# Rotary halves swapped by copies out of PSUM, the compression's sums moved forward, and the first head tile in the filling bank, in a two-layer hybrid attention kernel

## The chip, the cores and the metric

One core of one Trainium2 chip runs the whole program. The metric is the device time of one launch in microseconds (us): 1656.5 us is the median of 3 runs of the kernel before (1655.12 to 1657.21). Engines are named as the profile names them: PE (TensorE, matmul; PEld its weight loads), DVE (VectorE), ACT (ScalarE), POOL (GpSimd) and SP (SyncE, which here only issues DMAs).

## The reference, cut to what matters

Two layers of a hybrid block on 512 tokens of 1024 channels, all in float32. Only the part around the change is shown; the second attention (stick breaking), the merge and the convolutional feed-forward stay as they are.

```python
def rope(x, positions):                       # halves of 32 channels of each 64-channel head
    x1, x2 = xf[..., :half], xf[..., half:]
    return concatenate([x1 * cos - x2 * sin, x2 * cos + x1 * sin])

def compress_blocks(k, pe, w1, b1, w2):       # blocks of 32 tokens, stride 16
    blocks = k[:, idx] + pe
    return gelu(flat @ w1 + b1) @ w2

def hybrid_mixer(h, ...):
    q_nsa, kv_nsa, g_nsa, qkv_sb, g_merge = split(h @ w_in)
    q_nsa, k_cmp, k_slc, k_win = (rope(...) for the 8 query heads and 3 x 2 key heads)
    o_nsa = nsa_attention(...)                # compressed + selected + window branches, gated
    o_sb = stick_breaking_attention(...)
    return (sigmoid(g_a) * (o_nsa @ w_proj_nsa) + sigmoid(g_b) * (o_sb @ w_proj_sb)) @ w_out

for l in range(2):
    x = x + rms_norm(hybrid_mixer(rms_norm(x)))
    x = x + rms_norm(conv_ffn(rms_norm(x)))
```

## The kernel before, in words

Activations lie with channels on the 128 partitions and the 512 tokens along the free axis. Every large matmul is done as three (high times high, low times high, high times low), after a split of each 128x1024 block of weights into whi (ACT, L105) and wlo (DVE or POOL, L106). All matmuls are recorded at L382, in the helper `mm`; a projection of one 128x512 output tile is a "gemm" of 24 matmuls. So the trace is best read by tile names.

A layer starts with six **head tiles**, whose matmuls go in two halves of the tokens: two key tiles k1 and k2 (L644 and after, `k_tile`), two query tiles (`q_tile`), the compression's key tile (`kc_done`) and its value tile (written to `kd` at L677). They take the six PSUM banks of the pool `pg` (tag "bk"). Ahead of the loop the list of banks is turned by one (L565): the first head tile gets the second bank, and the last one gets the first.

Then come, in PE's order: `acc4`, four banks of 24 matmuls of 280 columns each (values and gate logits, 96 matmuls); two more query tiles (two gemms); and `cps`, two banks with 32 small matmuls each 132 columns wide, which sum the compression's windows from `cst`, the split copy of `cstk` (L712 ACT, L713 DVE). `cstk` is filled from `kd` by DMAs that SP issues (L660).

**rope** (L610) is run for seven tiles per layer, 14 in all. ACT copies the 128x512 bank to `rf` in SBUF (L616), which frees the bank once the copy is read out; SP issues four DMAs that write the four 32-partition blocks to `rs` in swapped order (L619); DVE multiplies `rf` by the cosines (L620) and, later, `rs` by the sines (L623); then sums and splits for k or q follow.

From the compression on, the attention is interleaved with **filling gemms**: projections for the second attention (`sb_pair`, read out by DVE at L781 as sbz) and for the merge's gates (`gate`, read out by DVE at L802). They all use one PSUM bank with the tag "f", the filling bank, so that a filling gemm can only start when the last one's bank has been read. The norm's sums in front of a layer use that tag, too, and in the second layer the last down-projection tiles of layer 0 (read by ACT at L1260) use the bank tags that the head tiles take over.

`cps` is read by ACT (`cpart`, L738), then by DVE (L739 and L740, `csum`), for two values of v in turn; `cpart` has one buffer.

The order of instructions on each engine isn't the order of the code: a scheduler sorts the recorded instructions by due times and costs, and `tc.high_priority()` pulls what is recorded in it forward. Each engine then runs its own list in order. When the bank a tile uses, or a priority, is changed, rows move on all engines, in the attention behind the change as well.

Lines that the steps below speak of: L561 `bank`, L564 and L565 the list of banks, L610 to L630 `rope`, L704 to L708 the reads of acc4 (vN, gates), L712 and L713 cst, L735 to L740 cpart and csum, L781 and L802 the reads of the filling bank, L859 to L870 the softmax of the compressed branch (cp, cm).

Of the kernel before, what the change touches and what calls it, by code (L numbers as in the profile page):

```python
# [9 lines left out]
F = mybir.dt.float32  # L10
# [20 lines left out]
HEAD = 6  # L31
# [127 lines left out]
def run_kernel(ctx, tc, xT, pos, inv, vec, pew, cw1, w_m, w_vn, w_pr, w_o, w_u, w_d, xmid, rot, out):  # L159
    nc = tc.nc  # L160
    uid = [0]

    def nm(s):
        uid[0] += 1
        return f"{s}_{uid[0]}"
# [56 lines left out]
    def act(out_, in_, fn, **kw):  # L222


        load_table(fn)
        op = nc.scalar.activation(out_, in_, fn, **kw)  # L226
        after(op, table["load"])
        table["users"].append(op)
# [134 lines left out]
    @contextmanager  # L363
    def temps(n):

        nonlocal tp_, n_tmp
        with pool("tp") as p:
            tp_, n_tmp = p, n
            yield p

    def wk(name, dt=F):
        return tp_.tile([128, T], dt, name=name, tag="tmp", bufs=n_tmp)
# [11 lines left out]
    def fbank(name):  # L384
        return ps1.tile([128, T], F, name=nm(name), tag="f" if name == "f" else "g", bufs=1)
# [138 lines left out]
    for l in range(DEPTH):  # L524
# [35 lines left out]
        def bank():  # L560
            return pg.tile([128, T], F, name=nm("bk"), tag="bk", bufs=6)  # L561


        banks = [bank() for _ in range(HEAD)]  # L564
        banks = banks[1:] + banks[:1]  # L565
        with temps(0) as hp:
            if l == 0:
                W.ensure(1)
# [12 lines left out]
        with temps(6) as ip:  # L581
# [6 lines left out]
            cosT, sinT = cs_t[:, 0], cs_t[:, 1]  # L588
# [21 lines left out]
            def rope(b, done):  # L610


                f = wk(nm("rf"))
                s_ = wk(nm("rs"))
                t = wk(nm("rt"))
                nc.scalar.copy(f, b)  # L616
                for p in range(4):
                    q = p ^ 1
                    nc.sync.dma_start(s_[p * 32:p * 32 + 32], f[q * 32:q * 32 + 32])  # L619
                nc.vector.tensor_mul(t, f, cosT)  # L620

                def rest():
                    nc.vector.tensor_mul(s_, s_, sinT)  # L623
                    done(t, s_)

                later.append(rest)

            def q_tile(p, b):
                def done(o, s_):
                    nc.vector.tensor_add(o, o, s_)  # L630
                    for e in range(2):
                        r = slice(e * 64, e * 64 + 64)
                        ro = slice(64 - e * 64, 128 - e * 64)
                        d = qs(2 * p + e)
                        nc.scalar.activation(d[r], o[r], AF.Copy, scale=0.125)
                        nc.vector.scalar_tensor_tensor(d[ro], o[r], 0.125, d.bitcast(F)[r], op0=OP.mult,
                                                       op1=OP.subtract)

                rope(b, done)

            def k_tile(br, b):
                def done(o, s_):
                    nc.vector.tensor_add(o, o, s_)
                    o = o.rearrange("p (j k) -> p j k", j=4)  # L644
                    for g in range(2):
                        r = slice(g * 64, g * 64 + 64)
                        ro = slice(64 - g * 64, 128 - g * 64)
                        hi, lo = (kdup(g, part).rearrange("p (j b k) -> p j b k", j=4, b=2)[:, :, br]
                                  for part in range(2))
                        nc.scalar.copy(hi[r], o[r])  # L650
                        nc.vector.tensor_sub(lo[r], o[r], hi.bitcast(F)[r])
                        both = kst[g].bitcast(F).rearrange("p (a b k) -> p a b k", a=8, b=2)[:, :, br]
                        nc.sync.dma_start(both[ro], both[r])

                rope(b, done)
# [11 lines left out]
            for i in head_second(banks, kept, n_pre=HEAD):  # L667
                b = banks[i]
                if i < 2:
                    k_tile(i, b)  # L670
                elif i < 4:
                    q_tile(i - 2, b)
                elif i == 4:
                    rope(b, kc_done)
                else:
                    mr = lambda a: a.rearrange("p (m r) -> p m r", r=2)
                    nc.vector.tensor_mul(kd[:, 1].rearrange("p r m -> p m r"), mr(b), mr(r2))  # L677
                    spread(1)
                flush_later(1)
# [5 lines left out]
            for n_kt in (3, 3, 2):  # L685
                hi, lo = W.get()
                for j in range(4):
                    tk = slice(j * 128, j * 128 + 128)
                    for q in range(n_kt):
                        a, b = hi[:, q * 280:q * 280 + 280], lo[:, q * 280:q * 280 + 280]  # L690
# [25 lines left out]
            for p in (2, 3):  # L716
                b = bank()
# [4 lines left out]
            cps = [bank(), bank()]  # L722
# [10 lines left out]
            hrep = aux[:, 320:576].rearrange("p (g a n) -> p g a n", g=2, a=4)  # L733
            nc.gpsimd.tensor_copy(aux[:, :192], PW[:64, 32:])
            for v in range(2):  # L735
                part = ip.tile([64, 132], F, name=nm("cpart"), tag="cpart")
                sums = ip.tile([64, 66], F, name=nm("csum"), tag="csum")
                nc.scalar.copy(part, cps[v][64:128, :132])  # L738
                nc.vector.tensor_add(part, cps[v][:64, :132], part)  # L739
                nc.vector.tensor_add(sums, part[:, :66], part[:, 66:])  # L740
                hb = ip.tile([64, 1], F, name=nm("hb"))
                nc.vector.tensor_add(hb, sums[:, 64:65], b1(v))
                act(hid[:, v], sums[:, 0:64], AF.Gelu_apprx_tanh, bias=hb)
# [384 lines left out]
        with temps(5) as yt:  # L1128
# [7 lines left out]
            with pool("py", space=PSUM) as py:  # L1136
# [18 lines left out]
                for m in projection(gb, s_hi, s_lo):  # L1155
                    t = wk(nm("yb"))
# [7 lines left out]
                def out_tile(m, tr, wt, side=None):  # L1164
                    b = bank()
                    w_ = tr.stop - tr.start
                    drain(gemm(b[:, :w_], wt, *y_of(tr), range(KD)), side)
                    return b[:, :w_]
# [10 lines left out]
                for m in range(n0):  # L1179
                    b = out_tile(m, ALL, W.get())  # L1180
# [3 lines left out]
                for m in range(n0, 8):  # L1184
                    kept[m] = W.get()
                    b = out_tile(m, HALVES[0], kept[m])
# [7 lines left out]
                for i, m in enumerate([6, 7, 2, 3, 4, 5]):  # L1194
                    b = out_tile(m, HALVES[1], kept[m], side)
# [11 lines left out]
            banks = [bank() for _ in range(HEAD)]  # L1207
# [9 lines left out]
        with temps(5) as ft_:  # L1217
# [24 lines left out]
            for i in range(HEAD, 2 * NF):  # L1242
                b = bank()
# [114 lines left out]
```

## Time and profile before

| what | value |
|---|---|
| median of 3 runs | 1656.5 us (1655.12 to 1657.21) |
| the profiled execution | 1653.88 us, of which the span on the engines is 1652.2 us; mean granted TensorE clock 0.989 |
| PE busy | 1609.0 us (97% of the span), 8970 matmuls |
| DVE, ACT, POOL busy | 1118.2 us (68%), 825.3 us (50%), 211.1 us (13%) |
| chain that ended last | PE 82%, DVE 8%, ACT 5%, DMA 2% |
| granted TensorE clock in 40 slices | 9 or more everywhere, but a little lower in the third slice (82 to 124 us) |
| DMA | 159.42 MB, mean 96 GB/s; 56 rotary swaps of 64 KB among them |

How to read it: PE is the bound. Since its instructions are in a fixed list, time is only lost where PE waits (an idle time in its timeline, with what released it) or where it runs at a lower granted clock (the clock column of a window: 1.00 is 2.4 GHz, 0.50 is 1.2 GHz). The busy time of another engine matters only where PE waits for it. Stretches named below: layer 0's head, acc4 and query tiles 28 to 80 us, its compression and attention 80 to 280 us; layer 1's the same from about 828, 895 us on.

### The profile page before, as it was taken

The numbers are of one execution on the slowest core, as the hardware profiler recorded it, in microseconds if no ns is written. First come the engines' busy times: TensorE is split into PE (matmuls) and PEld (weight loads), VectorE is DVE, ScalarE is ACT, GpSimd is POOL, SyncE is SP. The second block draws the span as 40 slices with busy tenths as digits, with TensorE's granted clock in tenths as the row PEclk, the third lists the DMA queues.
The fourth block names the chain that finished last, engine by engine and source line by source line (L and its number), as shares of the span: only waits on it lengthen the run. The fifth ranks groups of instructions, "written<-read, shape, count | busy, mean of one in ns | idle before, by whom it ended". The sixth has DMA issues, their size and how long they took to land.

```text
span 1652.2 us, 23212 instructions
## 1 busy us (share of the span) xinstructions
PE 1609.0 (97%) x8970; PEld 1393.2 (84%) x8970; DVE 1118.2 (68%) x1659; ACT 825.3 (50%) x1338; POOL 211.1 (13%) x252
## 2 busy tenths in 40 slices
PE   9899999999999999999999999999999999999997
PEld 9878887888998888888998788878889988888896
DVE  8775676767578777733677666677676687776235
ACT  6555565654555444423555455575536454444233
POOL 0034442120000000000000453322200000000000
PEclk9989999999999999999999999999999999999999
DMA  6521112114412233333664211112153132322344
GB/s 228 152 77 52 39 39 64 52 64 141 132 61 88 91 102 91 97 93 107 195 204 129 71 44 47 39 64 64 52 180 114 39 99 93 102 91 95 98 128 141
DMA packets 53501, 159.42 MB, mean 96 GB/s; under 512 B 6544, under 2 KB 12176, under 8 KB 53392
## 3 DMA queue, kind: packets, MB, share of 16 engines
q1 hardware_dynamic: 51088, 152.00, 29.0%
q0 software_dynamic: 1296, 4.72, 0.8%
q8 instruction: 70, 1.15, 0.3%
q10 hardware_dynamic: 1008, 1.23, 0.3%
q14 instruction: 39, 0.32, 0.1%
HBM read 144.30 MB, written 4.72 MB: 90 GB/s over the span
## 4 chain that ended last, share of the span: by engine, by line
PE 82%; DVE 8%; ACT 5%; issue 2%; DMA 2%; POOL 1%; SPq 1%; ACTq 0%; DVEq 0%; POOLq 0%
PE bk L382 56%; PE f L382 15%; PE pv L382 3%; PE Z L382 3%; PE S L382 2%; PE tp L935 2%; POOL sbt L1034 1%; DVE wlo L106 1%; DVE st L906 1%; DMA rs<-rf 1%; DMA x<-in_xT 1%; ACT whi L105 0%; ACT sbt L226 0%; ACT sbt L1058 0%; ACT sbw L226 0%
## 5 line engine op out<-in xcount | busy, mean ns | idle before, releaser
L105 ACT CAST whi<-wraw 128x1024 fp32r<-128x1024 f32 (+2 forms) x235 | 241.2, 1027 | 342.7 <-PE bk L382 254.3
L106 DVE TENSOR_TENSOR wlo<-wraw,whi 128x1024 fp32r<-128x1024 f32 (+2 forms) x209 | 248.8, 1191 | 184.1 <-ACT whi L105 181.4
L382 PE MATMUL bk<-h_hi,whi 128*128 128x512 f32 (+1 forms) x768 | 286.5, 374 | 2.1 <-ACT f_t L1260 1.7
L382 PE MATMUL bk<-h_hi,wlo 128*128 128x512 f32 (+1 forms) x768 | 286.4, 374 | 0.0
L382 PE MATMUL bk<-h_lo,whi 128*128 128x512 f32 (+1 forms) x768 | 286.2, 373 | 0.0
L382 PE MATMUL f<-h_hi,whi 128*128 128x512 f32 x448 | 184.4, 412 | 11.7 <-DVE gate L802 9.2
L382 PE MATMUL f<-h_lo,whi 128*128 128x512 f32 x448 | 179.1, 400 | 0.0
L382 PE MATMUL f<-h_hi,wlo 128*128 128x512 f32 x448 | 178.6, 399 | 0.0
L382 PEld LDWEIGHTS bk<-h_hi,whi 128*128 128x128 f32 x768 | 145.6, 190 | 27.7 <-ACT f_t L1260 1.9
L382 PEld LDWEIGHTS bk<-h_hi,wlo 128*128 128x128 f32 x768 | 145.5, 190 | 25.4 <-DVE wlo L106 0.4
L382 PEld LDWEIGHTS bk<-h_lo,whi 128*128 128x128 f32 x768 | 145.6, 190 | 24.8
L382 PE MATMUL bk<-ah,wlo 128*128 128x256 f32 (+1 forms) x484 | 161.7, 334 | 2.4 <-DVE wlo L106 2.4
L382 PE MATMUL bk<-ah,whi 128*128 128x256 f32 (+1 forms) x484 | 160.4, 331 | 0.0
L382 PE MATMUL bk<-al,whi 128*128 128x256 f32 (+1 forms) x484 | 160.2, 331 | 0.0
L382 PEld LDWEIGHTS f<-h_hi,whi 128*128 128x128 f32 x448 | 86.4, 193 | 30.6 <-DVE gate L802 10.0
L382 PEld LDWEIGHTS bk<-ah,wlo 128*128 128x128 f32 x484 | 91.8, 190 | 12.5 <-DVE wlo L106 3.4
L1228 DVE TENSOR_TENSOR cu<-bk,r 128x512 f32<-128x512 f32 x88 | 60.2, 687 | 61.2 <-PE bk L382 60.9
L382 PEld LDWEIGHTS f<-h_hi,wlo 128*128 128x128 f32 x448 | 85.9, 192 | 18.5
L382 PEld LDWEIGHTS f<-h_lo,whi 128*128 128x128 f32 x448 | 86.5, 193 | 15.5
L382 PEld LDWEIGHTS bk<-ah,whi 128*128 128x128 f32 x484 | 91.9, 190 | 8.7
L382 PEld LDWEIGHTS bk<-al,whi 128*128 128x128 f32 x484 | 91.9, 190 | 8.7
L382 PE MATMUL bk<-h_hi,wh 128*128 128x256 f32 x512 | 96.0, 285 | 0.0
(241 smaller groups left out, 3174.3 us busy)
## 6 DMA issues: line engine op xcount, KB each, us to landing
wraw<-in_w_u SPq DMA_DIRECT2D x88, 512.0 KB, 3.5
wraw<-in_w_m SPq DMA_DIRECT2D x72, 512.0 KB, 3.3
wraw<-in_w_d SPq DMA_DIRECT2D x44, 512.0 KB, 3.5
wraw<-in_w_d SPq DMA_DIRECT2D x22, 384.0 KB, 3.1
wraw<-in_w_pr SPq DMA_DIRECT2D x16, 512.0 KB, 3.6
wraw<-in_w_o SPq DMA_DIRECT2D x16, 512.0 KB, 3.5
rs<-rf SPq DMA_DIRECT2D x56, 64.0 KB, 2.8
wraw<-in_cw SPq DMA_DIRECT2D x4, 512.0 KB, 4.6
```

Source lines behind the costliest of these rows:

```text
L105: self.nc.scalar.copy(hi[:, c], raw[:, c])
L106: eng.tensor_sub(lo[:, c], raw[:, c], hi.bitcast(F)[:, c])
L382: last_mm[0] = nc.tensor.matmul(o, a, b, start=first, stop=last, skip_group_check=True)
L906: nc.vector.tensor_reduce(self.st[:, 0:2], self.S[:, :self.n].rearrange("p (j b k) -> p b j k", j=self.i + 1, b=2), axis=AX.XY, op=OP.max, ...
L935: nc.tensor.transpose(tp[:, b * 128:(b + 1) * 128], self.P[:, (c + b) * 128:(c + b + 1) * 128], ident)
L1034: nc.gpsimd.affine_select(out=d, in_=d, compare_op=OP.is_gt, fill=0.0, base=0, pattern=[[1, 128]], channel_multiplier=-1)
L1228: nc.vector.tensor_mul(u, b, r2)
```

## The change

Three edits. (1) rope drops `rf` and the DMAs: four ACT copies of 32 partitions each read the bank in swapped order and write `rs`, and DVE's multiplication by the cosines reads the bank itself. The bank is free when the copies and the multiplication have read it. (2) The first head tile goes into the filling bank, so that only five of the six banks are taken, and the list isn't turned. (3) `cpart` gets two buffers, and its copy and sum are recorded with high priority. Lines below the first edit move up by 1 to 3 (L619 and L620 become L616 and L617, L704 is L701, L712 is L709, L738 is L736, L781 is L779, L802 is L800, L863 is L861, L906 is L904).

```diff
--- before.py
+++ after.py
@@ -561,8 +561,7 @@
             return pg.tile([128, T], F, name=nm("bk"), tag="bk", bufs=6)
 
 
-        banks = [bank() for _ in range(HEAD)]
-        banks = banks[1:] + banks[:1]
+        banks = [fbank("f")] + [bank() for _ in range(HEAD - 1)]
         with temps(0) as hp:
             if l == 0:
                 W.ensure(1)
@@ -610,14 +609,12 @@
             def rope(b, done):
 
 
-                f = wk(nm("rf"))
                 s_ = wk(nm("rs"))
                 t = wk(nm("rt"))
-                nc.scalar.copy(f, b)
                 for p in range(4):
                     q = p ^ 1
-                    nc.sync.dma_start(s_[p * 32:p * 32 + 32], f[q * 32:q * 32 + 32])
-                nc.vector.tensor_mul(t, f, cosT)
+                    nc.scalar.copy(s_[p * 32:p * 32 + 32], b[q * 32:q * 32 + 32])
+                nc.vector.tensor_mul(t, b, cosT)
 
                 def rest():
                     nc.vector.tensor_mul(s_, s_, sinT)
@@ -733,10 +730,11 @@
             hrep = aux[:, 320:576].rearrange("p (g a n) -> p g a n", g=2, a=4)
             nc.gpsimd.tensor_copy(aux[:, :192], PW[:64, 32:])
             for v in range(2):
-                part = ip.tile([64, 132], F, name=nm("cpart"), tag="cpart")
+                part = ip.tile([64, 132], F, name=nm("cpart"), tag="cpart", bufs=2)
                 sums = ip.tile([64, 66], F, name=nm("csum"), tag="csum")
-                nc.scalar.copy(part, cps[v][64:128, :132])
-                nc.vector.tensor_add(part, cps[v][:64, :132], part)
+                with tc.high_priority():
+                    nc.scalar.copy(part, cps[v][64:128, :132])
+                    nc.vector.tensor_add(part, cps[v][:64, :132], part)
                 nc.vector.tensor_add(sums, part[:, :66], part[:, 66:])
                 hb = ip.tile([64, 1], F, name=nm("hb"))
                 nc.vector.tensor_add(hb, sums[:, 64:65], b1(v))
```

**ACT, layer 0, from the first rotary copy on.** bk_116 to bk_119 (before) and f_115, bk_116, bk_117 (after) are head tiles, in that order; bk_733 to bk_736 (before) and bk_723, bk_724 (after) are acc4's banks. Before:

```order
L616 COPY rf_507<-bk_116 128x512
L616 COPY rf_545<-bk_117 128x512
L616 COPY rf_591<-bk_118 128x512
L650 CAST kst_5_105<-rt_509 64x4x128
L650 CAST kst_6_106<-rt_509 64x4x128
L616 COPY rf_638<-bk_119 128x512
L650 CAST kst_5_105<-rt_547 64x4x128
L650 CAST kst_6_106<-rt_547 64x4x128
L704 ACTIVATE vN_732<-bk_733,rT_465 128x4x64
L704 ACTIVATE vN_732<-bk_734,rT_465 128x4x64
```

Now:

```order
L616 COPY rs_507<-f_115 32x512 x4
L701 ACTIVATE vN_722<-bk_723,rT_465 128x4x64
L616 COPY rs_543<-bk_116 32x512 x4
L701 ACTIVATE vN_722<-bk_724,rT_465 128x4x64
L705 ACTIVATE gates_111<-bk_723,rT_465 128x24
L616 COPY rs_587<-bk_117 32x512 x4
L647 CAST kst_5_105<-rt_508 64x4x128
```

The first two reads of acc4 (vN) and a gates read stand between the copies of the first three tiles now; before, they stood behind four tiles' copies and the splits of the keys.

**SP, layer 1, around the compression's DMAs (cstk).** Before:

```order
L653 DMA kst_743_7536<-kst_743_7536 64x8x128
L619 DMA rs_8017<-rf_8016 32x512 x4
L660 DMA cstk_7805<-kd_7810 64x256 x6
L74 DMA wraw_8288<-in_w_m 128x1024
L660 DMA cstk_7805<-kd_7810 64x256 x2
L619 DMA rs_8224<-rf_8223 32x512 x4
L619 DMA rs_8258<-rf_8257 32x512
```

Now:

```order
L657 DMA cstk_7791<-kd_7796 64x256 x4
L74 DMA wraw_8151<-in_w_m 128x1024
L650 DMA kst_735_7521<-kst_735_7521 64x8x128
L650 DMA kst_736_7522<-kst_736_7522 64x8x128
L650 DMA kst_735_7521<-kst_735_7521 64x8x128
L650 DMA kst_736_7522<-kst_736_7522 64x8x128
L657 DMA cstk_7791<-kd_7796 64x256 x4
L74 DMA wraw_8260<-in_w_m 128x1024
L74 DMA wraw_9516<-in_w_m 128x1024
```

The swaps (rs) are gone from the list. The second group of cstk stands behind issues for the keys (kst), ahead of the weights wraw_8260; before, it was split, with the weights wraw_8288 between its parts and four swaps ahead of it.

**DVE, layer 0, the softmax of the compressed branch and the reads of the filling bank.** f_2343 (before) and f_2329 (now) are the same filling gemm, the first for a gate; f_2305 and f_2291 are the one ahead of it. Before:

```order
L860 TENSOR_TENSOR cp_1093<-cp_1093,cm_1096 128x512
L922 TENSOR_TENSOR st_1127<-st_1127,gates_111 128x2
L863 TENSOR_REDUCE cm_1096<-cp_1093 128x16
L864 RECIPROCAL cm_1096<-cm_1096 128x16
L867 TENSOR_TENSOR cm_1096<-cm_1096,gates_111 128x16
L802 TENSOR_TENSOR gate_2342<-f_2343,r_90 128x512
L868 TENSOR_TENSOR cm_1096<-cm_1096,rowv 128x16
L906 TENSOR_REDUCE st_1166<-S_1137 128x2
L870 TENSOR_TENSOR cp_1093<-cp_1093,cm_1096 128x512
```

Now:

```order
L861 TENSOR_REDUCE cm_1082<-cp_1079 128x16
L779 SCALAR_TENSOR_TENSOR sbz_2322<-f_2291,r_90 128x512
L904 TENSOR_REDUCE st_1152<-S_1123 128x2
L862 RECIPROCAL cm_1082<-cm_1082 128x16
L904 TENSOR_REDUCE st_1173<-S_1162 128x2
L787 TENSOR_TENSOR sbst_2250<-sbz_2322,sbst_2250 64x512
L865 TENSOR_TENSOR cm_1082<-cm_1082,gates_111 128x16
L787 TENSOR_TENSOR sbst_2250<-sbz_2322,sbst_2250 64x512
L919 RECIPROCAL st_1152<-st_1152 128x2
L866 TENSOR_TENSOR cm_1082<-cm_1082,rowv 128x16
L920 TENSOR_TENSOR st_1152<-st_1152,gates_111 128x2
L868 TENSOR_TENSOR cp_1079<-cp_1079,cm_1082 128x512
```

PE's list has also moved there. Before, f_2343 was followed by the scores S_1137 and S_1176 and the next filling gemm; now:

```order
L382 LDWEIGHTS identb
L382 MATMUL S_1123<-cbias,identb 128x256
L382 MATMUL S_1162<-kst_5_105,qst_4_104 128x512 x2
L382 LDWEIGHTS identb
L382 MATMUL S_1162<-cbias,identb 128x256
L382 MATMUL pv_1136<-pt_1032,vN_722 128x256
L382 MATMUL pv_1136<-pt_1033,vN_722 64x256
L382 MATMUL pv_1136<-pt_1032,vN_722 128x256
L382 MATMUL pv_1136<-pt_1033,vN_722 64x256
L382 MATMUL f_2329<-h_hi,whi_2277 128x512
```

These scores stand ahead of the gemm f_2329 now, and the gemm waits for sbz_2322 (the read of the bank that f_2291 filled), which stands on DVE behind the row sum of cp (L861), where it once stood ahead of the whole softmax. The read of f_2329 (L800) is the row that follows the last one shown, behind the end of the softmax (L868).

## Rows read from the trace of the kernel before

**Rows 1.** The page: the span and the busy time of the engines.

```profile
span 1652.2 us, 23212 instructions
PE 1609.0 (97%) x8970; PEld 1393.2 (84%) x8970; DVE 1118.2 (68%) x1659; ACT 825.3 (50%) x1338; POOL 211.1 (13%) x252
```

**Rows 2.** The timeline of PE at the ends of its idle times in the two stretches that the change touches (48 to 126 us and 828 to 941 us); start and length in us, and in brackets how long PE had been idle and which instruction released it.

```profile
48.47 0.50 PE L382 MATMUL bk<-wh,h_hi 128*128 128x280 f32 x2 [2.38 <-ACT wh L92]
79.82 0.41 PE L382 MATMUL bk<-cst,wh 128*128 128x132 f32 x2 [1.88 <-DVE cst L713]
120.19 0.80 PE L382 MATMUL f<-h_hi,whi 128*128 128x512 f32 x1 [4.01 <-DVE gate L802]
828.29 0.39 PE L382 MATMUL bk<-h_hi,whi 128*128 128x256 f32 x1 [1.67 <-ACT f_t L1260]
894.96 0.41 PE L382 MATMUL bk<-cst,wh 128*128 128x132 f32 x2 [1.56 <-DVE cst L713]
935.34 0.80 PE L382 MATMUL f<-h_hi,whi 128*128 128x512 f32 x1 [4.01 <-DVE gate L802]
```

**Rows 3.** Windows: the stretch in us, its length, the busy us of PE, PEld, DVE, ACT and POOL (instructions in brackets), the granted clock of TensorE, the DMA share and GB/s.

```profile
48.20:78.60 30.40, 29.32 (x168) 25.93 (x168) 23.45 (x39) 15.69 (x28) 0.33 (x2) 1.00 0.60 163
48.50:54.00 5.50, 5.50 (x43) 5.50 (x44) 2.34 (x3) 0.85 (x2) 0.33 (x2) 1.00 0.79 265
61.50:77.90 16.40, 16.40 (x73) 13.24 (x71) 15.79 (x27) 10.46 (x20) 0.00 (x0) 1.00 0.60 150
79.80:88.00 8.20, 8.18 (x38) 7.76 (x39) 6.90 (x10) 4.93 (x8) 0.34 (x1) 0.58 0.43 131
120.20:126.00 5.80, 5.80 (x15) 4.60 (x16) 2.09 (x6) 1.02 (x4) 1.04 (x1) 0.57 0.26 90
828.30:834.00 5.70, 5.70 (x46) 5.65 (x47) 3.34 (x4) 2.67 (x3) 0.00 (x0) 1.00 0.80 285
858.00:893.00 35.00, 35.00 (x223) 32.20 (x222) 27.74 (x44) 17.21 (x30) 0.33 (x2) 1.00 0.61 173
895.00:903.00 8.00, 8.00 (x39) 7.42 (x40) 7.68 (x12) 4.97 (x8) 0.59 (x1) 0.60 0.45 142
935.30:941.00 5.70, 5.66 (x13) 4.46 (x14) 2.14 (x6) 1.02 (x4) 1.04 (x1) 0.50 0.26 93
```

**Rows 4.** Groups of the rotary lines, L616 to L620: nanoseconds least/median/most and the first and last start in us; under L616 what ACT waited for ahead of it (us, times).

```profile
L616 ACT COPY rf<-bk x14: 567/588/621, 48.3 to 888.7; 128x512 f32<-128x512 f32 x14
  DMA rs<-rf: 9.5, 3
...
L619 SPq DMA_DIRECT2D rs<-rf x56: 507/588/1296, 49.6 to 894.5; - x56
...
L620 DVE TENSOR_TENSOR rt<-rf,cs_t x14: 680/690/708, 49.5 to 890.3; 128x512 f32<-128x512 f32 x14
```

**Rows 5.** Groups of lines whose operations are near to the new ones: a read of PSUM by DVE, and ACT reads of fewer partitions or columns; columns as in the group above.

```profile
L802 DVE TENSOR_TENSOR gate<-f,r x32: 670/688/693, 119.5 to 1180.0; 128x512 f32<-128x512 f32 x32
L766 ACT CAST vc<-cb x8: 255/258/259, 104.2 to 921.6; 32x128 fp32r<-32x128 f32 x8
L704 ACT ACTIVATE vN<-bk,rT x8: 468/476/486, 61.7 to 879.6; 128x256 fp32r<-128x256 f32 x8
```

**Rows 6.** The timeline of DVE, ACT and SP (its DMA issues) ahead of PE's idle times at 48, 79 and 895 us.

```profile
47.26 1.06 DVE L677 TENSOR_TENSOR kd<-bk,r 128x512 f32<-128x512 f32 x1
48.28 1.07 ACT L616 COPY rf<-bk 128x512 f32<-128x512 f32 x2
70.66 1.28 ACT L635 ACTIVATE qst<-rt 64x512 fp32r<-64x512 f32 x2
73.11 1.07 ACT L105 CAST whi<-wraw 128x1024 fp32r<-128x1024 f32 x1
77.36 1.18 ACT L712 CAST cst<-cstk 128x528 fp32r<-128x528 f32 x1 [2.70 <-DMA cstk<-kd]
78.57 1.11 DVE L713 TENSOR_TENSOR cst<-cstk,cst 128x528 fp32r<-128x528 f32 x1 [0.26 <-ACT cst L712]
880.37 7.30 SPq L660 DMA_DIRECT2D cstk<-kd  x6
888.34 1.10 SPq L660 DMA_DIRECT2D cstk<-kd  x2
892.49 1.18 ACT L712 CAST cst<-cstk 128x528 fp32r<-128x528 f32 x1 [3.18 <-DMA cstk<-kd]
```

**Rows 7.** The timeline of ACT, DVE and POOL ahead of PE's idle time that ends at 120.19 us.

```profile
115.52 0.63 ACT L226 ACTIVATE cp<-cp 128x512 f32<-128x512 f32 x1 [1.29 <-DVE cp L860]
116.18 0.69 DVE L863 TENSOR_REDUCE cm<-cp 128x16 f32<-128x512 f32 x1 [0.63 <-ACT cp L226]
117.19 2.34 DVE L867 TENSOR_TENSOR cm<-cm,gates 128x16 f32<-128x16 f32 x1
117.16 2.34 POOL L106 TENSOR_TENSOR wlo<-wraw,whi 128x1024 fp32r<-128x1024 f32 x1 [0.40 <-ACT whi L105]
119.45 0.68 DVE L802 TENSOR_TENSOR gate<-f,r 128x512 f32<-128x512 f32 x1
```

**Rows 8.** The waits: who waited for what, us in total, times, the longest.

```profile
ACT cpart L738 <- DVE csum L740: 4.2, 2, 2.1
PE tp L935 <- DVE pt L946: 2.1, 2, 1.0
```

## The prediction

> **What bounds the kernel.** I read the page first: PE is busy for 1609.0 of 1652.2 us [rows 1], so the kernel can only gain where PE idles or runs at a lower clock. Then I read PE's timeline for its idle times. In the stretches that the change touches, six of them count [rows 2]: 2.38 us before acc4 in layer 0 (48.47), 1.88 and 1.56 us before the compression's sums (79.82 and 894.96), twice 4.02 us before a filling gemm that waits for the read of its bank (120.19 and 935.34), and 1.67 us before layer 1's first head tile (828.29). Together 15.5 us. The windows behind them show a second cost [rows 3]: the granted clock falls to about half, 1.2 instead of 2.4 GHz, behind both sums and both gate waits. (1 - 0.58) x 8.2 = 3.4 us are lost at 79.8, 2.5 us at 120.2, 3.2 us at 895 and 2.85 us at 935.3. It doesn't fall behind the waits that end at 48.47 and 828.29: the windows after them show 1.00. So 27.5 us lie in places that this change can reach. Everything else of the edit has to be judged by whether it makes PE wait anew.
>
> **The rope by itself: no direct gain.** What goes: per tile one ACT copy of 0.588 us and four SP issues of 0.588 us (33 us of SP's time in all) [rows 4]. PE never waits for either; ACT waited for the swaps for 9.5 us, and is busy for only half of its time. What comes: four ACT copies of 32x512 out of PSUM, for which the trace has no row. From below, a copy of 32x128 takes 0.257 us [rows 5], so four cost at least 1.03 us. From above, the 128x512 copy takes 0.588 us, four of them 2.35 us, if partitions count for nothing and nothing overlaps. Two such copies in a row took 1.07 us [rows 6], so each further one adds 0.48, and I take 0.588 + 3 x 0.48 = 2.03 us: the column count is that of the row at 0.588. DVE's multiplication reads PSUM now; a DVE pass over such a bank takes 0.688 us, over SBUF 0.690 [rows 4, 5]: nothing. ACT gets 14 x (2.03 - 0.59) = 20 us, 10 per layer. Cover: ACT is busy for 15.7 of 30.4 us between 48.2 and 78.6, and for 17.2 of 35 us in layer 1's query stretch [rows 3]. It fits, but the room is gone if a copy takes much more than 0.6 us (a rival below). A bank is held for 2.03 + 0.69 = 2.7 us instead of 0.59; with one more bank free that falls on one place only, next.
>
> A rule of the Trainium skill speaks against the edit ("ScalarE: Activation LUTs", What ACT_TABLE_LOAD costs): an activation costs a fixed part and a time per column, and overlaps the next one a little. Partitions don't enter, so four copies of a quarter's height cost what four full ones do. By its figures (186 ns + 0.833 ns a column, less 93 ns of overlap) four take 2.17 us, an estimate, and ACT would get 22 us instead of 20. No row here shows a 32x512 copy.
>
> **Layer 0, before acc4: 2.38 becomes about 1.4.** The wait was for DVE, which read the value tile's bank until 48.3 (L677) [rows 6]; the label wh is an instruction done long before PE could go on. Now acc4's first bank is the free sixth, so PE goes on at 46.1. A bank is 24 matmuls, 24 x 5.5/43 = 3.1 us [rows 3], so its first two are done at 49.2 and 52.2 (the second takes the value tile's bank, free at 48.3). The third takes the first one's bank again, and its reads stand on ACT (the order shown for ACT): copies 48.3 to 50.3, vN of 0.48 to 50.8 [rows 5], copies to 52.8, vN to 53.3, gates (24 columns, by the 0.257 of 128 columns) to 53.6. PE waits for 1.4: -1.0 us. Bounds: 0 and -2.4.
>
> **Layer 0, the compression's sums: 1.88 becomes about 1.2.** PE's work from acc4 to here is unchanged, 79.82 - 1.88 - 48.47 = 29.5 us, so the filling gemm in front ends at 46.1 + 29.5 + 1.4 = 77.0. ACT's list from the end of the second query gemm (one gemm is 16.4/3 = 5.5 us earlier [rows 3], at 71.5): whi 1.07, four copies 2.03, qst 1.28, cst 1.18 [rows 6], to 77.1; DVE's half of cst, 1.11, to 78.2. PE waits for 1.2: -0.7 us. The lower clock behind it I leave as it is, since an idle of this kind stays; bounds 0 and -0.7 - 3.4.
>
> **Layer 1, first head tile: -1.7 us.** It takes the filling bank and no longer waits for ACT's L1260. Late next would be the split weights; bounds 0 and -1.7. Its acc4 then has the same third bank as in layer 0: between 0 and +1.4, since there is no table to finish and ACT is less behind; I take +0.6.
>
> **Layer 1, the compression's sums: -4.8 us.** In this layer cst waited for DMAs: SP needed 7.3 us for six cstk issues and sent the last two only at 888.3, and ACT's split began at 892.5 [rows 6]. The tile's key sum no longer waits for a swap, and by ACT's list cst stands ahead of the last query tile's copies, some 7 us earlier. The wait goes (1.56), and with it the lower clock (3.2). Bounds 0 and -4.8.
>
> **The attention, moved by the scheduler.** The gate wait: the filling gemm f_2343 was done at 116.2, but the read of its bank stood on DVE behind the softmax, where L867, a 128x16 operation, took 2.34 us beside POOL's wlo [rows 7]. Now the softmax is put ahead: scores stand before the gemm, and DVE's rows up to L868 lie beside its 5.5 us. What is late next is the gemm's start, which waits for sbz behind L861, two passes of 0.69 after the exponential: between 0 and 1.4, I take 0.8. So 2 x (4.0 - 0.8) = -6.4 us, and the lower clock goes at both places: -5.3 us. Bounds 0 and -13.3. Against that, the first filling gemm of the attention now has scores ahead of its last matmul, and its bank is read behind two score reductions of 0.69 each, so PE waits there for 0.9 us per layer (bounds 0 and 1.4): +1.8. Everything else of the attention up to 280 us is shuffled too. Waits such as tp for pt are there now (2.1 us in two) [rows 8], and the same kinds will come at other places: between -2 and +3 us per layer, I take +1 each: +2.
>
> **Priority for cpart.** Its second copy no longer waits for csum, 4.2 us in two on ACT [rows 8]. PE has 5.5 us of filling gemm beside it: no direct gain.
>
> **Sum.** -1.0 - 0.7 - 1.7 + 0.6 - 4.8 - 6.4 - 5.3 + 1.8 + 2.0 = -15.5. From the profiled execution's 1653.9 us that is 1638.4; the median of the runs shown stands 2.6 us above that execution, so 1641.0 us.
>
> **Rivals.**
> 1. *The waits shrink, but the clock falls all the same*, at layer 1's sums and both gate places. For it: idles of 0.8 to 1.4 stay near them, and the lowest idle that the clock fell behind is 1.56. Against: 1.67 and 2.38 didn't lower it. -15.5 + 3.2 + 5.3 = -7.0: 1649.5.
> 2. *Layer 0's sums keep the full clock too*: -15.5 - 3.4, 1637.6. For it: the idle there is shorter than any behind which the clock fell.
> 3. *The gate wait stays*: POOL's wlo again lies beside DVE's softmax (2.34 us instead of some 0.25) and the bank's read stands behind its whole chain now. -15.5 + 6.4 + 5.3 = -3.8: 1652.7.
> 4. *Slower: ACT becomes what the query stretch waits for*, if a 32x512 copy is dearer than a full one. Without its seven copies ACT has some 11.6 us of work between 48.2 and 78.6, and 13.1 in layer 1's window; 28 copies of c us fill the stretches at c = 0.67 and 0.78. Beyond that the sums start later by 28 us per us of c in each layer, and the gains up to there (8.2, less the 0.6) are gone, which leaves some -8. At c = 1.0 that is 9.2 + 6.2 = +15.4, +7.5 in all: 1664; the sign turns at c = 0.87. For it: no row has this shape, and seven tiles hold their banks longer. Against: no ACT row grows with fewer partitions.
> 5. *The edit does nothing*: PE had other reasons to wait at every place, 1656.5.
>
> **Numbers.** A measurement of this kernel can tell about 0.2%, 3.3 us, from no change. Forecast 0.55, rival 1 0.13, rival 2 0.13, rival 3 0.09, rival 4 0.06, rival 5 0.04. Faster by more than that: the forecast, rivals 1 and 2 and a third of rival 3, 0.84. Within it: two thirds of rival 3 and rival 5, 0.10. Slower: 0.06. The range takes in rival 2 with 3 us of the attention's bounds, 1634.5, and on the other side rival 1 with as much, 1652.5; it leaves out most of rival 3 and rivals 4 and 5.
>
> **What would show it.** Right: no idle at 828 and before layer 1's sums, clock 1.00 in layer 1's 895 to 903; acc4 begins at 46.1 and has one idle of about 1.4 before its third bank; copies of about 0.55 us, four in a row in 2.0; the two idles of 4.02 replaced by some of under 1 us at 1.00. Wrong: copies over 0.67 us; a low clock behind the short idles; a gate read that PE waits for by over 2 us; idle times in the rest of the attention that grow by over 3 us per layer.

## The result, and the profile after

The changed kernel takes 1643.27 us (median of 4 runs, 1642.83 to 1643.96); the kernel before has 1656.45 beside it. The ratio is 0.9922, 95% interval 0.9904 to 0.9939: faster by 13.2 us. The forecast was 1641.0, range 1634.5 to 1652.5. The profiled executions differ by 11.05 us (1653.88 and 1642.83). The other 2.1 us come from where these two executions lie: that of before 2.6 us under its median, that of the change 0.4 us.

The page, against [rows 1]: PE is busy for 5.8 us less with the same number of matmuls, so part of the gain is clock, and ACT has 26 us more.

```profile
span 1640.9 us, 23136 instructions
PE 1603.2 (98%) x8970; PEld 1388.6 (85%) x8970; DVE 1111.5 (68%) x1659; ACT 851.3 (52%) x1380; POOL 210.3 (13%) x252
```

PE's timeline, the idle times at the places of [rows 2] and the new ones; start and length in us, in brackets how long PE had been idle and what released it:

```profile
54.70 0.53 PE L382 MATMUL bk<-wh,h_hi 128*128 128x280 f32 x2 [2.04 <-ACT gates L705]
81.40 0.77 PE L382 MATMUL bk<-cst,wh 128*128 128x132 f32 x5 [2.35 <-DVE cst L710]
95.59 0.50 PE L382 MATMUL f<-h_hi,whi 128*128 128x512 f32 x1 [0.90 <-DVE sbz L779]
114.71 0.49 PE L382 MATMUL f<-h_hi,whi 128*128 128x512 f32 x1 [1.03 <-DVE sbz L779]
...
894.42 0.51 PE L382 MATMUL S<-kst,qst 128*128 128x256 f32 x2 [2.55 <-DVE cpart L737]
903.36 0.47 PE L382 MATMUL f<-h_hi,whi 128*128 128x512 f32 x1 [0.88 <-DVE st L919]
922.33 0.50 PE L382 MATMUL f<-h_hi,whi 128*128 128x512 f32 x1 [0.97 <-DVE sbz L779]
```

Both gate waits of 4.01 us (in front of the filling gemm behind the compressed softmax, called the gate place from here on) have become about 1 us, and layer 1's first head tile waits for nothing. The two waits in layer 0's rotary stretch are as long as before (2.04 and 2.35, where 2.38 and 1.88 were), and layer 1 has a new one of 2.55. The windows behind these places, columns as in [rows 3]; the granted clock is the third number from the end:

```profile
54.70:60.00 5.30, 5.30 (x29) 5.30 (x30) 4.60 (x10) 5.14 (x9) 0.00 (x0) 0.68 0.00 1
81.40:89.60 8.20, 8.20 (x39) 7.62 (x40) 6.04 (x14) 3.35 (x8) 0.37 (x1) 0.60 0.31 96
114.70:120.00 5.30, 5.29 (x23) 4.39 (x24) 4.26 (x10) 2.25 (x6) 3.25 (x2) 1.00 0.30 99
887.30:891.30 4.00, 4.00 (x35) 3.94 (x34) 3.17 (x6) 2.10 (x4) 0.34 (x1) 1.00 0.36 131
895.00:899.00 4.00, 3.96 (x11) 3.10 (x11) 3.52 (x10) 2.38 (x4) 0.00 (x0) 0.57 0.50 121
922.30:928.00 5.70, 5.67 (x25) 4.71 (x26) 4.27 (x10) 2.35 (x7) 3.26 (x2) 1.00 0.29 92
```

The clock holds behind both gate places now (0.57 and 0.50 before), and during layer 1's sums. It falls anew behind acc4's wait in layer 0 (5.3 x 0.32 = 1.7 us) and behind layer 1's new wait (4.0 x 0.43 = 1.7 us).

Where the gate wait went is read on DVE and POOL, against [rows 7]:

```profile
113.24 0.69 DVE L861 TENSOR_REDUCE cm<-cp 128x16 f32<-128x512 f32 x1 [0.37 <-ACT cp L226]
113.96 0.69 DVE L779 SCALAR_TENSOR_TENSOR sbz<-f,r 128x512 f32<-128x512 f32 x1
...
115.99 1.18 DVE L787 TENSOR_TENSOR sbst<-sbz,sbst 64x512 fp32r<-64x512 f32 x1
117.20 0.18 DVE L865 TENSOR_TENSOR cm<-cm,gates 128x16 f32<-128x16 f32 x1
...
120.50 0.69 DVE L800 TENSOR_TENSOR gate<-f,r 128x512 f32<-128x512 f32 x1 [1.41 <-PE f L382]
114.22 2.40 POOL L106 TENSOR_TENSOR wlo<-wraw,whi 128x1024 fp32r<-128x1024 f32 x1 [0.78 <-ACT whi L105]
```

The softmax now ends while the gemm runs, and the gate's read (L800) waits for PE, where PE waited for it. POOL's wlo is as long as before, and the DVE operation that lasts longer beside it is another one (L787, 1.18 us; 0.69 when the same line runs again at 117.41, with POOL idle); the multiplication of the 128x16 tile takes 0.18 us, not 2.34.

### The profile page after: what moved, and what is told of

Its sections match the earlier page's. It is cut to its first block, busy times and chain, and to the rows that moved or that the text cites. A ratio compares the mean times of both kernels' runs of the same rounds, so it can differ in the third digit from the quotient of the medians.

```text
span 1640.9 us, 23136 instructions
## 1 busy us (share of the span) xinstructions
PE 1603.2 (98%) x8970; PEld 1388.6 (85%) x8970; DVE 1111.5 (68%) x1659; ACT 851.3 (52%) x1380; POOL 210.3 (13%) x252
## 4 chain that ended last, share of the span: by engine, by line
PE 89%; DVE 4%; ACT 4%; issue 1%; DMA 1%; SPq 0%; ACTq 0%; DVEq 0%
PE bk L382 58%; PE f L382 18%; PE Z L382 4%; PE pv L382 4%; PE S L382 2%; PE tp L933 2%; ACT rs L616 1%; ACT whi L105 1%; DMA cstk<-kd 1%; DVE wlo L106 0%; DVE st L904 0%; PE cs L382 0%; DVE qst L633 0%; DVE rs L462 0%; PE ms L436 0%
## 5 line engine op out<-in xcount | busy, mean ns | idle before, releaser
L382 PE MATMUL bk<-h_hi,wlo 128*128 128x512 f32 (+1 forms) x736 | 277.2, 377 | 0.1
L382 PE MATMUL bk<-h_hi,whi 128*128 128x512 f32 (+1 forms) x736 | 276.1, 375 | 0.2 <-ACT whi L105 0.2
L382 PE MATMUL bk<-h_lo,whi 128*128 128x512 f32 (+1 forms) x736 | 276.1, 375 | 0.0
L382 PE MATMUL f<-h_hi,whi 128*128 128x512 f32 (+1 forms) x480 | 192.7, 401 | 8.2 <-DVE sbz L779 2.9
L382 PE MATMUL f<-h_hi,wlo 128*128 128x512 f32 (+1 forms) x480 | 188.3, 392 | 0.0
L382 PE MATMUL f<-h_lo,whi 128*128 128x512 f32 (+1 forms) x480 | 187.4, 391 | 0.0
L382 PEld LDWEIGHTS bk<-h_hi,wlo 128*128 128x128 f32 x736 | 138.4, 188 | 25.6 <-DVE wlo L106 0.3
L382 PEld LDWEIGHTS bk<-h_hi,whi 128*128 128x128 f32 x736 | 138.3, 188 | 25.4 <-ACT whi L105 0.4
L382 PEld LDWEIGHTS bk<-h_lo,whi 128*128 128x128 f32 x736 | 138.5, 188 | 24.6
L382 PEld LDWEIGHTS f<-h_hi,wlo 128*128 128x128 f32 x480 | 91.9, 191 | 17.9 <-DVE wlo L106 0.2
```

What stands on the lines that cost most here:

```text
L382: last_mm[0] = nc.tensor.matmul(o, a, b, start=first, stop=last, skip_group_check=True)
```

## The experiments

Two theories were on trial. Theory A: most of the gain is the gate wait with the clock behind it, and only the order of DVE's rows decides it. Theory B: the gain is made where the edits are, by the copies and the bank in the rotary stretch. Ratios are to the kernel before on the same chip; the ranges in us were given for its 1656.5. It took 1657.90 on the chip of the first four runs, 1656.14 on that of gate_alone, busy_wait, split16 and copy_forms, and 1657.24 on that of the others.

**Undo one edit: priority.**

```diff
-                with tc.high_priority():
-                    nc.scalar.copy(part, cps[v][64:128, :132])
-                    nc.vector.tensor_add(part, cps[v][:64, :132], part)
+                nc.scalar.copy(part, cps[v][64:128, :132])
+                nc.vector.tensor_add(part, cps[v][:64, :132], part)
```

(and cpart has one buffer again). 

> The change without its third edit (priority for cpart): the rotary copies and the first head tile in the filling bank stay. In its order of instructions the read of the filling bank for the first gate stands behind the compressed softmax in both layers, as in the kernel before. Theory A (most of the gain is the gate wait and the lower clock behind it, and only the order of rows decides it): the two idles of about 4 us and two stretches at half clock come back, 2 x (3.0 + 3.4) = 12.9 us, and the time is 1654 to 1657. Theory B (the gain is made by the copies and the bank in the rotary stretch, and the priority is a detail that only saves ACT a wait): 1643 to 1646.

Measured: 1653.44 us, ratio 0.9971 (0.9959 to 0.9983). The time is just under theory A's range. Without the priority most of the gain is gone. PE's timeline shows why: both gate waits are back, and layer 1 has one more.

```profile
121.46 0.80 PE L382 MATMUL f<-h_hi,whi 128*128 128x512 f32 x1 [3.45 <-DVE gate L799]
900.07 0.77 PE L382 MATMUL f<-h_hi,whi 128*128 128x512 f32 x1 [3.68 <-DVE sbz L778]
935.75 0.79 PE L382 MATMUL f<-h_hi,whi 128*128 128x512 f32 x1 [3.75 <-DVE gate L799]
```

**Undo one edit: rope.** L616 to L620 as before (ACT copy to rf, four DMAs, multiplication of rf).

```diff
+                f = wk(nm("rf"))
...
+                nc.scalar.copy(f, b)
...
-                    nc.scalar.copy(s_[p * 32:p * 32 + 32], b[q * 32:q * 32 + 32])
-                nc.vector.tensor_mul(t, b, cosT)
+                    nc.sync.dma_start(s_[p * 32:p * 32 + 32], f[q * 32:q * 32 + 32])
+                nc.vector.tensor_mul(t, f, cosT)
```

> The change without its first edit: swaps by DMA as before, first head tile in the filling bank, priority for cpart. In its order layer 0's first gate read stands ahead of the compressed softmax, layer 1's still stands behind it. Theory A: one gate wait with its slow stretch (6.4 us) goes, one stays, and the idle at layer 1's first head tile goes (1.7); with 0 to 2 us from acc4's wait, 1645 to 1649. Theory B: without the copies the waits for cst and acc4 stay as they were and the time is 1653 to 1656.

Measured: 1650.99 us, 0.996 (0.9946 to 0.9975), between the two theories and outside both ranges. Layer 0's gate wait did go, as its order said, but the new order has its own wait, of 5.42 us, at a filling gemm in front; layer 1's gate wait stays:

```profile
80.76 0.77 PE L382 MATMUL f<-h_hi,whi 128*128 128x512 f32 x1 [5.42 <-DVE sbz L781]
933.90 0.80 PE L382 MATMUL f<-h_hi,whi 128*128 128x512 f32 x1 [3.75 <-DVE gate L802]
```

**Undo one edit: the bank.**

```diff
-        banks = [fbank("f")] + [bank() for _ in range(HEAD - 1)]
+        banks = [bank() for _ in range(HEAD)]
+        banks = banks[1:] + banks[:1]
```

> The change without its second edit: rotary copies and priority, but all six head tiles in the pool's banks. In its order the first gate read stands behind the softmax in layer 0 and in layer 1. Theory A: both gate waits and both slow stretches stay, so 1652 to 1657; layer 1's first head tile waits for the bank as before. Theory B: the copies make the gain, 1644 to 1648.

Measured: 1650.46 us, 0.9954 (0.9937 to 0.997): 1.5 us under theory A's range and 2.5 us above B's, so neither holds here. A wait of about 4 us is at the same place in both layers, in layer 1 for sbz instead of the gate:

```profile
123.58 0.79 PE L382 MATMUL f<-h_hi,whi 128*128 128x512 f32 x1 [3.74 <-DVE gate L801]
928.95 0.80 PE L382 MATMUL f<-h_hi,whi 128*128 128x512 f32 x1 [4.03 <-DVE sbz L780]
```

**The first edit alone.** The rope lines of the change, the rest as before. 

> Only the first edit: rotary copies out of PSUM instead of swaps by DMA. Theory A: order of the gate reads as before, so both gate waits stay; ACT gets 14 x (2.35 - 0.59) = 25 us that are mostly hidden: 1652 to 1658. Theory B: 1644 to 1650.

Measured: 1649.21 us, 0.9947 (0.9928 to 0.9965), inside theory B's range. It has waits of 3.75 and 4.04 us at the gate places. So theory A erred in giving the copies nothing: they are worth some 8.7 us by themselves (6 to 12 by the interval). In this order layer 1's sums wait for nothing (1.56 before), and the clock doesn't fall there (3.2): the step that the forecast had for the whole change.

```profile
121.82 0.80 PE L382 MATMUL f<-h_hi,whi 128*128 128x512 f32 x1 [3.75 <-DVE gate L800]
891.65 3.69 PE L382 MATMUL bk<-cst,wh 128*128 128x132 f32 x32
925.65 0.80 PE L382 MATMUL f<-h_hi,whi 128*128 128x512 f32 x1 [4.04 <-DVE sbz L779]
```

The priority added to the rope alone changes nothing that can be told (that is the kernel no_bank, 1650.46), while the same priority added to the other two edits is worth some 8 us (no_prio to the change, 0.9971 to 0.9922). So what an edit is worth depends on the order that comes of all of them.

**The gate place alone, with none of the edits.** One weight block's low half goes from POOL to DVE:

```diff
-            it(w_m[l, i], eng=nc.vector if i in (8, 9, 10) else nc.gpsimd)
+            it(w_m[l, i], eng=nc.vector if i in (8, 9, 10, 17) else nc.gpsimd)
```

> The kernel before with none of the three edits: only the low half of one weight block per layer (wlo of the second gate's gemm, w_m block 17) is split on DVE instead of POOL. By its order this puts the read of the first gate's bank right behind the row sum of the compressed softmax (L863), ahead of the slow L867, in both layers; the rotary stretch and PE's list up to there are as before. Theory A (the gate wait with the clock behind it is most of the gain): the two idles of 4.0 us shrink to about 1 and the two slow stretches of 3.4 us go: 2 x 6.4 = 12.8 us less the 1.2 us that DVE's split takes, so 1644 to 1648 where the kernel before has 1656.5. Theory B (a wait at this place costs little, since PE's list is filled elsewhere, and the gain comes from the copies and the bank): 1653 to 1657.

Measured: 1644.59 us, 0.9929 (0.9915 to 0.9944). That is as fast as the change, without any of it: the gate place alone can give the whole gain, as theory A has it, though rope_only shows that the copies can gain by themselves too. DVE reads the gate's bank right behind the row sum, PE's wait is 0.52 and 0.48, and the clock holds:

```profile
118.52 0.50 PE L382 MATMUL f<-h_hi,whi 128*128 128x512 f32 x1 [0.52 <-DVE gate L802]
930.19 0.50 PE L382 MATMUL f<-h_hi,whi 128*128 128x512 f32 x1 [0.48 <-DVE gate L802]
117.18 0.69 DVE L863 TENSOR_REDUCE cm<-cp 128x16 f32<-128x512 f32 x1 [0.63 <-ACT cp L226]
117.78 0.68 DVE L802 TENSOR_TENSOR gate<-f,r 128x512 f32<-128x512 f32 x1
119.68 0.91 DVE L867 TENSOR_TENSOR cm<-cm,gates 128x16 f32<-128x16 f32 x1
```

```profile
118.50:124.30 5.80, 5.78 (x25) 4.78 (x26) 3.19 (x8) 1.17 (x5) 3.10 (x2) 1.00 0.30 90
```

**Both gains at once.** The first edit, and blocks 16 and 17 in the list above. 

> Only the first edit (rotary copies), with the low halves of two weight blocks per layer (w_m blocks 16 and 17, the first two gates' gemms) split on DVE instead of POOL. In its order both first gate reads stand right behind the softmax's row sum. Theory A (the gate waits and the copies' own gains are separate and add up): the copies alone gave about -8 us, the moved splits alone -11.6; the copies' kernel still had one gate wait of 3.75 us, one sbz wait of 4.0 us and 5.1 us of clock at these places, so these 11 us go: 1636 to 1640. Theory B (the copies' gain was itself a shift of the attention's waits, and no more than one of the two gains can be had): 1643 to 1645.

Measured: 1636.51 us, 0.9874 (0.9858 to 0.989). Theory A's range holds: the copies' 8.7 us and the gate place's 11.6 add up (20.7 measured, with one more block moved). In layer 0 PE doesn't idle at all where it waited for the gate, and the clock is 1.00; in layer 1 a wait of 0.32 us for sbz is left. Behind acc4's wait the clock fell:

```profile
105.00:125.00 20.00, 20.00 (x105) 16.38 (x104) 15.46 (x35) 8.73 (x21) 5.91 (x6) 1.00 0.25 80
...
48.60:54.00 5.40, 5.08 (x27) 5.11 (x28) 3.82 (x6) 5.26 (x10) 0.80 (x2) 0.68 0.84 290
```

**Is it the idle time that lowers the clock?** In the changed kernel, ahead of layer 0's sums:

```diff
+            if l == 0:
+                dm = fbank("dm")[:, :264].rearrange("p (a b) -> p a b", a=4)
+                for _ in range(10):
+                    mm(dm, h_hi[:, 0, :128], cst[:, 0, 0, 0:4, :66], True, True)
             cps = [bank(), bank()]
```

> The changed kernel with ten matmuls of 264 columns added in layer 0 behind the filling gemm and ahead of the compression's sums; they read the high half of the late cst tile, write a bank that nobody reads, and no other instruction moves. They lie in the idle of 2.35 us, which shrinks to about 0.7 and 0.1 in two parts. Theory A (the clock falls because PE idles): the stretch behind it stays at 1.00; the sums take 3.7 us as they do in layer 1 instead of 5.6, and the filling gemm behind them is at full clock: 2 to 3.5 us less, 1640 to 1641. Theory B (it falls for the small matmuls of the sums themselves, or with the time of day): clock as before, 1643 to 1644.

Measured: 1640.24 us, 0.9905 (0.989 to 0.992), some 3 us faster than the change (which has 1643.27, on another chip; the two intervals overlap). PE idles for 1.53 us, then runs the added matmuls, and the sums start when cst is ready, as before. They take 3.8 us, where they take 5.6 in the changed kernel, and the window behind is at 1.00 (0.60 there):

```profile
80.06 1.50 PE L382 MATMUL dm<-cst,h_hi 128*128 128x264 f32 x10 [1.53 <-ACT cst L709]
81.47 3.79 PE L382 MATMUL bk<-cst,wh 128*128 128x132 f32 x32
```

```profile
81.50:90.00 8.50, 8.50 (x55) 7.66 (x55) 5.92 (x14) 4.96 (x10) 0.53 (x1) 1.00 0.34 93
```

The sums start as late as in the change (81.47 and 81.40), and PE's next wait ends at 92.41 us instead of 95.59, so the 3.2 us are gained between the two. So matmuls whose output nobody reads are worth some 3 us here, while the wait for data is untouched. In all ten profiles without them in which PE waited for cst ahead of layer 0's sums (1.88 to 2.99 us) the clock fell behind it; in the two with them it held.

The same ten matmuls in the kernel rope_split: 

> As the kernel rope_split, with the ten matmuls in the idle ahead of layer 0's sums that the run busy_wait had. Theory A: a further 2 to 3 us, as there: 1634 to 1637. Theory B (in another order of the rows the clock falls elsewhere instead): as rope_split.

Measured: 1633.58 us, 0.9859 (0.9844 to 0.9874), the fastest of all: 2.9 us under rope_split, some 10 under the change by the ratios, 23.7 under the kernel before. That is a little below theory A's range.

**One split moved in the changed kernel** (16 added to the list above). 

> The changed kernel with the low half of one weight block per layer (w_m block 16, the first gate's gemm) split on DVE instead of POOL. In its order the read of the filling bank ahead of that gemm (sbz) no longer stands behind the softmax's row sum. Theory A: the idles of 1.03 and 0.97 us there go, and nothing comes in their place: 1640 to 1642. Theory B (any change of the order moves the waits about, and what goes at one place comes at another): 1643 or more.

Measured: 1641.47 us, 0.9907 (0.9891 to 0.9924). The wait of 1.03 went to 0.54. That of 0.97 went, but a wait for vc just ahead of it grew from 0.21 to 0.68, and the one ahead of layer 0's sums from 2.35 to 2.83, as theory B has it. 

> The kernel of run split16 once more, one look, for how far its single run lies from its median of 1641.5: 1640 to 1643.

This single run took 1644.8 us. With that the 1.8 us of split16 against the change aren't shown; both theories stay open for it.

**The form of the copies.** 

> The changed kernel with other forms of ACT's copies in the first three head tiles (their keys and queries are then not rotated rightly): tile 1 four 32x512 copies that don't swap partitions; tile 2 four 128x128 copies side by side; tile 3 four 32x256 copies of four partition blocks, four 32x64 copies of the same block, and two larger ones. The other tiles copy as in the change, 0.588 us each, four in 2.35 us, without the overlap of 0.1 us that two copies of 128x512 from two banks showed. Theory A (a copy that starts on other partitions than the one ahead doesn't overlap it): tile 1 takes 2.35 too, tile 2's four copies overlap by 0.1 each (about 0.26 + 3 x 0.17 = 0.8), and the four 32x64 copies overlap. Theory B (two reads of the same bank don't overlap): no form overlaps, tile 2 takes 4 x 0.26 = 1.0 or more. Theory C (the crossing of partitions costs it): tile 1 overlaps and takes 2.0.

Of its edit, in short (each line stands in a loop over the four p; tile 3's two larger copies and the copies of the other tiles, which are those of the change, aren't shown):

```diff
+                if kind == 0:      # 32x512, partitions not swapped
+                    nc.scalar.copy(s_[p * 32:p * 32 + 32], b[p * 32:p * 32 + 32])
+                elif kind == 1:    # 128x128
+                    nc.scalar.copy(s_[:, p * 128:p * 128 + 128], b[:, p * 128:p * 128 + 128])
+                elif kind == 2:    # 32x256 of four blocks, then 32x64 of one block
+                    nc.scalar.copy(s_[p * 32:p * 32 + 32, :256], b[p * 32:p * 32 + 32, :256])
+                    nc.scalar.copy(s_[0:32, 256 + p * 64:320 + p * 64], b[0:32, 256 + p * 64:320 + p * 64])
```

Its time (1648.5, one run) says nothing, since the order has moved. ACT's timeline, start and length of each four:

```profile
48.70 2.34 ACT L620 COPY rs<-f 32x512 f32<-32x512 f32 x4
...
51.56 0.76 ACT L623 COPY rs<-bk 128x128 f32<-128x128 f32 x4
52.18 1.48 ACT L626 COPY rs<-bk 32x256 f32<-32x256 f32 x4
53.67 0.52 ACT L628 COPY rs<-bk 32x64 f32<-32x64 f32 x4
...
57.95 2.35 ACT L634 COPY rs<-bk 32x512 f32<-32x512 f32 x4
```

Crossing partitions costs nothing (2.34 and 2.35), and reads of one bank do overlap: four 128x128 copies take 0.76 and four 32x64 copies of the same block 0.52, at some 0.28 and 0.2 us each. Copies that start on another block than the one ahead don't: 1.48 is four times 0.36 with 0.01 us between. Theory A of this run holds.

## Why the prediction was right, by its own steps

**Right: the attention's gate wait.** Forecast -6.4 us of idle and -5.3 of clock; measured 8.02 to 2.00, -6.0, and 1.00 in both windows, where 2.5 and 2.85 were lost [rows 3]. This is nearly the whole of the change: gate_alone takes the same wait away with none of the three edits, and gains 11.6 us. Right, too, was what is late next: sbz behind the row sum, 1.0 us where 0.8 was taken. The new wait for the filling bank at the attention's start is 0.90 and 0.88 us, where 0.9 was forecast; in layer 1 it hangs on another read (st) than on the one named.

**Right: layer 1's head.** The 1.67 us in front of it [rows 2] are gone, and its acc4 waits for nothing (0.6 was taken).

**Wrong in size: the copies.** 2.03 us for four was forecast from the overlap of two 128x512 copies; it is 2.35, the bound from above, since copies that change their block don't overlap (copy_forms). The group of the copies out of the banks bk; then the first tile's four copies, and further down ACT's half of cst, which waits for its DMA:

```profile
L616 ACT COPY rs<-bk x48: 575/579/583, 51.6 to 888.9; 32x512 f32<-32x512 f32 x48
```

```profile
48.76 2.35 ACT L616 COPY rs<-f 32x512 f32<-32x512 f32 x4
78.53 1.17 ACT L709 CAST cst<-cstk 128x528 fp32r<-128x528 f32 x1 [0.36 <-DMA cstk<-kd]
```

ACT got 26 us instead of 20. The estimate by the Trainium skill ("ScalarE: Activation LUTs", What ACT_TABLE_LOAD costs) was 22; the overlap of 93 ns that the page gives isn't there when the copies change their block (2.35 us for four, where its figures give 2.17), so the measurement decides.

**Wrong: layer 0's rotary stretch**, -1.7 forecast with the clock as it was. Acc4 did begin without a wait, at 46.28 us (46.1 was forecast). Its third bank waits for 2.04 instead of 1.4: the two groups of copies are 0.6 longer (PE and ACT were both 0.5 later than forecast, which cancels). With that wait the clock fell, 1.7 us, which the forecast had not priced: acc4's wait of 2.38 had left the clock alone in the trace of before [rows 3]. This 1.7 belongs to the profiled execution and isn't shown to come with the change: in busy_wait and in both runs of split16 PE waits 2.07 to 2.15 us for the same release, and the window behind is at 1.00.

The sums wait for 2.35 instead of 1.2. The copies are 0.3 longer, but the step that failed is what cst waits for: the forecast put DVE's half of it right behind ACT's. ACT's half, 0.36 late for its DMA, ended at 79.70, and DVE began its own only at 80.25, when it was through with its rows for the rotary tiles, which stand ahead of it now:

```profile
79.64 0.69 DVE L627 TENSOR_TENSOR rt<-rt,rs 128x512 f32<-128x512 f32 x1
80.25 1.10 DVE L710 TENSOR_TENSOR cst<-cstk,cst 128x528 fp32r<-128x528 f32 x1
```

Net: 0.3 us less idle, 0.5 more, 1.7 of clock, so +1.9.

**Wrong: layer 1's sums**, -4.8 forecast. The wait for cst did go, and the sums run at 1.00. But what is late next was not asked. The scores stand right behind the sums now, and their bank is that of the sums, which cpart must read; ACT and DVE have the last query tile ahead of it:

```profile
887.09 2.35 ACT L616 COPY rs<-bk 32x512 f32<-32x512 f32 x4
889.47 0.69 DVE L617 TENSOR_TENSOR rt<-bk,cs_t 128x512 f32<-128x512 f32 x1 [0.75 <-ACT rs L616]
891.52 1.28 ACT L632 ACTIVATE qst<-rt 64x512 fp32r<-64x512 f32 x2 [2.08 <-DVE rt L627]
892.83 0.43 ACT L736 COPY cpart<-bk 64x132 f32<-64x132 f32 x2
...
893.62 0.29 DVE L737 TENSOR_TENSOR cpart<-bk,cpart 64x132 f32<-64x132 f32 x1
```

The sums end at 891, cpart is read from 892.83 on, and PE idles for 2.55 us; the clock falls behind it (1.7). What was gained (1.56 and 3.2) is given back but for 0.5 us. The rope alone has the full gain here, with a wait of 0.50 at this place.

**The rest of the attention** was taken at +2 us. The idle times over 0.2 us behind the gate places add up to 5.5 us per layer before and 5.0 after, so -1.0. Ahead of acc4 in layer 0 PE waited 0.6 us more, most of it for split weights (whi).

So -15.5 was forecast for the profiled execution and -11.05 measured. The two rotary stretches were over-priced by 3.6 and 4.3 us, the rest of the attention was priced 3.0 too high. The terms measured here add up to about -10, so some 1 us isn't placed. The time came closer than the sum (2.3 us off), since 2.6 us between execution and median were added, where the change's own execution lies only 0.4 under its median. That the forecast came so near is in part luck: its errors went both ways.

Of the rivals, the clock (1) was right for one place in a new guise: it fell, but behind other waits. Layer 0's sums didn't keep the full clock (2): 0.60. The gate wait didn't stay (3). ACT as the bound (4) didn't come: a copy takes 0.58 us, under the 0.67 that it needed. But the stretch was nearly full all the same: ACT was busy for 29.5 of 30.9 us from 48.8 to 79.7 in a window of the changed kernel. The priority was priced at nothing by itself. That holds where it is added to the rope alone, but through the order it decides over some 8 us.

## What to carry to other kernels

Where a scheduler sets the order, price an edit by the rows that move anywhere, and test the place that gains by itself: one moved operation gave here what three edits gave. Behind each wait that goes, ask who reads the bank that the next work needs; and where a wait for data can't go, matmuls that keep TensorE busy through it can save the clock. Copies of quarter height cost what full ones do, and they don't overlap when each starts on another block.

## What the runs showed of the hardware that was not expected

- ACT copies that start on another partition block than the one ahead don't overlap: 4 x 32x512 in 2.35 us, 4 x 32x256 in 1.48. On the same partitions they overlap by about 0.1 us: 4 x 128x128 in 0.76, 4 x 32x64 in 0.52.
- The clock doesn't fall behind every wait of a kind. Ahead of acc4 in layer 0 PE idled for 2.37 to 2.38 us in six kernels: the window behind is at 1.00 in the kernel before and in no_bank, and at 0.68 to 0.70 in rope_only, gate_alone, rope_split and rope_split_busy. Behind a wait of 1.42 us for pt in layer 1 (1047 us) it fell in one run of split16's kernel (0.65) and held in the other. What tells them apart isn't settled.
- Small matmuls pay nearly the whole price of the lower clock: the 32 matmuls of 132 columns take 3.69 us at 1.00 (rope_only, layer 1) and 7.06 where it is 0.50 throughout (gate_alone, layer 1). The 5.6 us of the changed kernel's layer 0 are at a mean of 0.65.

```profile
891.73 7.06 PE L382 MATMUL bk<-cst,wh 128*128 128x132 f32 x32 [2.21 <-DVE cst L713]
```

```profile
891.80:898.80 7.00, 7.00 (x33) 7.00 (x34) 6.74 (x10) 4.83 (x8) 0.49 (x1) 0.50 0.37 103
```

- A DVE operation on two SBUF tiles ended with POOL's operation beside it: 128x16 took 2.34 us beside POOL's 2.34 [rows 7], 0.91 where it began later beside such an operation (gate_alone), and 0.18 without it.
